# Low parts of the activations on VectorE, shorter chains, and own space for the split of h, in a hybrid attention block

## The chip, the cores and the metric

The kernel runs on one NeuronCore of a Trainium2 chip. The metric is the device time of one execution in microseconds (us), from which the median of several runs is taken. The core has five instruction queues: TensorE (PE in the profile, with its weight loads as PEld), VectorE (DVE), ScalarE (ACT), GpSimd (POOL) and SyncE (SP), which here only issues transfers. Each works its own queue in order and waits on the others through semaphores.

## What is computed

The reference is one layer of a hybrid block on x of 2048 tokens by 1024 features, in float32, cut here to what matters:

```python
u = rmsnorm(h, norm_w)
q, k, v, g, gate_lr, z, xbc, dt_raw = split_columns(u @ w_in)
gla_out = rmsnorm(gla_chunked(q, k, v, log_a), gla_norm_w) * silu(g)
xs, bm, cm = split(silu(causal_depthwise_conv(xbc)))
dt = softplus(dt_raw + dt_bias)
y = rmsnorm((ssd_chunked(xs, dt, a_neg, bm, cm) + xs * d_skip) * silu(z), ssd_norm_w)
h = h + concat(gla_out, y) @ w_out
h = h + sigmoid(rmsnorm(h, pe_norm_w) @ w_pe_gate) * (p @ w_pe)
return rmsnorm(h, final_norm_w)
```

`gla_chunked` is gated linear attention over four heads; `ssd_chunked` a state space scan over two groups of eight heads of width 64. In each chunk of the scan the state gains `B^T (x * dt * decay_to_end)`.

## The kernel before, in words

The tokens are worked in four blocks of 512 (`NB` = 4, `TB` = 512), each as four chunks of 128 (`NT` = 4). Features lie on the partitions, tokens along the free axis. Every large product is made of three passes of TensorE in a reduced float32 format: an operand is split into a **high part**, which is a copy rounded to that format, and a **low part**, the operand minus its high part, and the passes are high*high, high*low and low*high. So each activation that TensorE reads costs a copy (ScalarE) and then a subtraction that needs the copy. Weights are split in the first block (`split_w`, lines 196 and 197), written back to memory, and only loaded in the later three (`load_w`).

The steps that the change touches:
- `u_steps` (L379): the normalized input of the next block, eight pieces of 128 x 512. L386 multiplies (VectorE), L387 copies the high part (ScalarE), L389 forms the low part: GpSimd in general, VectorE for the even pieces of the first block.
- `gla_steps` (L513): one head of the gated attention. L559 and `rsqrt_tiny` give a scale per token, L563 applies it with four ScalarE passes (`on`), L569 transposes, L573 multiplies with the gate, L574 and L575 split into `mq`; L575 is GpSimd's. `mq` is read by the output projection (L878 to L880).
- `ssd_steps` (L580): one group of the scan. `make_x` (L599) transposes x of a chunk into a PSUM bank (L602), L604 (VectorE) makes `xd` = x * dt from it, L607 (GpSimd) makes `xe` = `xd` * dte, L611 (ScalarE) and L612 (GpSimd) split `xe` into `xh`. The state update L660 to L662 reads `xh`; L657 reads `xd`. `make_m` (L630) makes the decay mask, ten ScalarE passes (L634, L636) and two VectorE passes (L637) per chunk. L663 (GpSimd) scales the state.
- `ssd_norm_steps` (L676): L681, L683 and L684 normalize and split the scan's output; L684 is GpSimd's.
- `lr_steps` (L421) makes dt, the decays and `dte` in small tiles.
- The end of a block: `out_proj(ht, mqd, h_done)` (L1000) adds the last projection to h, feature tile by feature tile (d = 0 to 7). After each, `h_done` (L989) makes the high part (L995, ScalarE) and the low part (L996, VectorE) of h times a weight, and `hsq.add` squares h (L353, ScalarE) and sums the squares (L356, GpSimd). The tiles 0 to 3 go to one buffer of the tag `mq`, 4 to 7 to a second, and that tag has two buffers; at d = 4 the second one is still read as `mqd` by the projection under way. Then come the gate products (`dense_t`, L254 to L256), whose first one has the sum of squares (`sum_bc`, L320) behind its sixth feature tile (`mid`, L257).

The order of work on every engine comes from a scheduler, which starts from the order of the program and moves instructions that it holds ready past others. Side work (generators in `side`) is advanced by `step()` between the large products.

Of the kernel before, what the change touches and what calls it, by code (L numbers as in the profile page):

```python
# [35 lines left out]
def hybrid_kernel(ctx, tc, x_nat, x_t, p_t, w_t, w_n0, w_n, w_o, w_g, w_p, prm, gup, cst, out):  # L36
# [342 lines left out]
    def u_steps(b, rb, res, src=None):  # L379
        u = big.tile([P, 2, KT, TB], F32R, name="u", tag="u")  # L380
        res.append(u)
        for k in range(KT):
            xp = sb.tile([P, TB], F32, name="xp", tag="tmp", bufs=SB["tmp"])
            if src is None:
                nc.sync.dma_start(out=xp, in_=x_t[b, :, k, :])
            stt(out=xp, in0=xp if src is None else src[:, k, :], scalar=pr[:, C_NW + k:C_NW + k + 1], in1=rb, op0=ALU.mult, op1=ALU.mult)  # L386
            nc.scalar.copy(out=u[:, 0, k, :], in_=xp)  # L387
            eng = nc.gpsimd if src is None or k % 2 else nc.vector
            eng.tensor_tensor(out=u[:, 1, k, :], in0=xp, in1=u[:, 0, k, :].bitcast(F32), op=ALU.subtract)  # L389
            yield  # L390

    corr = []
# [28 lines left out]
    def lr_steps(lrn, lrT, dtr, cx):  # L421
# [49 lines left out]
        dte = sm.tile([P, NT, 16], F32, name="dte", tag="dte", bufs=1)  # L471
        tt(out=flat(dte), in0=cps[:, NS:2 * NS], in1=flat(cum), op=ALU.subtract)
        act(out=flat(dte), in_=flat(dte), func=AF.Exp)
        cx.update(dt=dt, cum=cum, elast=elast, dte=dte, cd=cd, ecd=ecd)

    def loga_steps(lrT, heads, bcs):
# [36 lines left out]
    def gla_steps(h, v, sg, fs, qm, km, mq):  # L513
# [46 lines left out]
        rs = rsqrt_tiny(ss, NT, 1.0 / 256, EPS)  # L560
        on = sb.tile([P, NT, 256], F32, name="on", tag="amh", bufs=SB["amh"])
        for t in range(NT):
            act(out=on[:, t, :], in_=rs_in[t // 2][:, (t % 2) * 256:(t % 2 + 1) * 256], func=AF.Copy,  # L563
                scale=rs[:, t:t + 1])
        yield
        for e2 in range(2):
            ps = pss.tile([P, TB], F32, name="pss")
            for t in range(NT):
                nc.tensor.transpose(out=ps[:, t * P:(t + 1) * P], in_=on[:, t, e2 * P:(e2 + 1) * P],  # L569
                                    identity=ident)  # L570
            kt = 2 * (h % 2) + e2
            og = sg[:, e2, :]
            stt(out=og, in0=ps, scalar=hgw[:, e2:e2 + 1], in1=og, op0=ALU.mult, op1=ALU.mult)  # L573
            nc.scalar.copy(out=mq[:, 0, kt, :], in_=og)  # L574
            nc.gpsimd.tensor_tensor(out=mq[:, 1, kt, :], in0=og, in1=mq[:, 0, kt, :].bitcast(F32),  # L575
                                    op=ALU.subtract)
            if e2 == 0:
                yield

    def ssd_steps(g, bt, ctl, xs, cx):  # L580
# [18 lines left out]
        def make_x(t):  # L599
            xps = pss.tile([P, TB], F32, name="pss")  # L600
            for m in range(4):
                nc.tensor.transpose(out=xps[:, m * P:(m + 1) * P], in_=xs[:, m, t * P:(t + 1) * P], identity=ident)  # L602
            xd = sb.tile([P, 8, 64], F32, name="xd", tag="xd", bufs=SB["xd"])
            tt(out=xd, in0=xps.rearrange("p (h c) -> p h c", c=64),  # L604
               in1=dt[:, t, h8].unsqueeze(2).broadcast_to([P, 8, 64]), op=ALU.mult)
            xe = sb.tile([P, 8, 64], F32, name="xe", tag="tmp", bufs=SB["tmp"])
            nc.gpsimd.tensor_tensor(out=xe, in0=xd, in1=dte[:, t, h8].unsqueeze(2).broadcast_to([P, 8, 64]),  # L607
                                    op=ALU.mult)
            xh = sb.tile([P, 2, 512], F32R, name="xh", tag="xh", bufs=SB["xh"])
            xef = xe.rearrange("p h c -> p (h c)")  # L610
            nc.scalar.copy(out=xh[:, 0, :], in_=xef)  # L611
            nc.gpsimd.tensor_tensor(out=xh[:, 1, :], in0=xef, in1=xh[:, 0, :].bitcast(F32), op=ALU.subtract)  # L612
            return xd, xh

        def load_m(t):
# [60 lines left out]
    def ssd_norm_steps(g, xs, sqs, mq):  # L676
# [3 lines left out]
        for m in range(4):  # L680
            stt(out=xs[:, m, :], in0=xs[:, m, :], scalar=pr[:, C_SW + 4 * g + m:C_SW + 4 * g + m + 1],  # L681
                in1=y, op0=ALU.mult, op1=ALU.mult)
            nc.scalar.copy(out=mq[:, 0, m, :], in_=xs[:, m, :])  # L683
            nc.gpsimd.tensor_tensor(out=mq[:, 1, m, :], in0=xs[:, m, :], in1=mq[:, 0, m, :].bitcast(F32), op=ALU.subtract)  # L684

    def final_steps(b, ht, parts, cs, deng, pool=()):
        n = cs.stop - cs.start
# [22 lines left out]
    def new_mq():  # L710
        return big.tile([P, 2, 4, TB], F32R, name="mq", tag="mq", bufs=2)
# [41 lines left out]
    for b in range(NB):  # L753
# [229 lines left out]
        if b + 1 < NB:  # L983
            gu = u_steps(b + 1, rbs.pop(), ures)
            side.append(gu)
        hw = [None, None]
        hsq = SumSq()

        def h_done(d):  # L989
            if d % 4 == 0:  # L990
                hw[d // 4] = new_mq()
            hd = ht[:, d, :]
            w = pr[:, C_PW + d:C_PW + d + 1]
            hq = hw[d // 4]
            act(out=hq[:, 0, d % 4, :], in_=hd, func=AF.Copy, scale=w)  # L995
            stt(out=hq[:, 1, d % 4, :], in0=hd, scalar=w, in1=hq[:, 0, d % 4, :].bitcast(F32),  # L996
                op0=ALU.mult, op1=ALU.subtract)
            hsq.add(hd)

        out_proj(ht, mqd, h_done)  # L1000
# [12 lines left out]
        for d, cs in jobs:  # L1013
# [6 lines left out]
            for k in range(2):  # L1020
# [3 lines left out]
                mm(out=pps, lhsT=hi[:, sl], rhs=pb[:, ks], start=(k == 0), stop=False)  # L1024
                mm(out=pps, lhsT=hi[:, sl], rhs=pl[:, ks], start=False, stop=False)
                mm(out=pps, lhsT=lo[:, sl], rhs=pb[:, ks], start=False, stop=(k == 1))
            gps = dense_t(lambda k: hw[k // 4][:, 0, k % 4, cs], lambda k: hw[k // 4][:, 1, k % 4, cs], n, gw[d],
                          None if yh else h_sum)
            if yh is None:
                yh = True  # L1030
# [101 lines left out]
```

## Time and profile before

| | us |
|---|---|
| median of 3 runs | 1877.78 (1873.1 to 1881.28) |
| the profiled execution | 1877.63 |
| its span in the profile | 1875.9 |
| PE busy | 1831.1 (98%) |
| PEld busy | 1538.6 (82%) |
| DVE busy | 1021.3 (54%) |
| ACT busy | 776.1 (41%) |
| POOL busy | 383.4 (20%) |

The span is the time from the first to the last instruction that the profile counts; the execution lasts 1.7 us longer. An engine's busy time is the union of its instructions. A matmul record lasts longer than the distance to the next, since they are pipelined, so time lost by PE is better seen in its waits and in the distances between starts. A wait names the instruction that released the engine.

### The profile page before, as it was taken

What the parts mean: (1) busy time and instruction counts of PE and PEld (TensorE: products, weight loads), DVE (VectorE), ACT (ScalarE), POOL (GpSimd) and SP (SyncE); (2) the same over time, 40 slices, a digit from 0 to 9 for tenths busy, and PEclk for the clock granted to TensorE, in tenths of its full rate; (3) what the DMA queues carried; (4) which work ended last, traced back from release to release, by engine and by line L of the source; (5) the groups of instructions that cost most, each with busy time, mean ns of one, the idle gap of its engine ahead of it and who ended that gap; (6) DMA issues with size and microseconds to landing.
All of it is one profiled execution on the core that took longest, in us unless ns stands there. A gap on an engine that the chain in (4) does not pass through costs nothing.

```text
span 1875.9 us, 25880 instructions
## 1 busy us (share of the span) xinstructions
PE 1831.1 (98%) x9674; PEld 1538.6 (82%) x9674; DVE 1021.3 (54%) x1959; ACT 776.1 (41%) x1557; POOL 383.4 (20%) x355
## 2 busy tenths in 40 slices
PE   8989999999999999999999999999999999999997
PEld 6878888877887888887788788887888888888887
DVE  8776676477566345425555544523546545551544
ACT  6575454355355334224434533313424453321431
POOL 3132012034203101204311310301420221020222
PEclk9999999999999999999999999999999999999998
DMA  7767686778785557556568556655657755666651
GB/s 271 266 214 268 225 304 217 267 245 286 256 285 162 185 164 235 161 180 214 181 225 251 154 172 197 203 176 176 217 178 264 214 157 169 182 196 187 204 174 46
DMA packets 131853, 390.60 MB, mean 208 GB/s; under 512 B 13712, under 2 KB 32400, under 8 KB 131344
## 3 DMA queue, kind: packets, MB, share of 16 engines
q1 hardware_dynamic: 129744, 382.39, 63.0%
q0 software_dynamic: 1984, 6.55, 0.9%
q8 instruction: 76, 1.25, 0.3%
q14 instruction: 49, 0.40, 0.1%
HBM read 306.58 MB, written 82.31 MB: 207 GB/s over the span
## 4 chain that ended last, share of the span: by engine, by line
PE 76%; DVE 5%; DMA 4%; ACT 3%; issue 2%; POOL 1%; SPq 0%; DVEq 0%; ACTq 0%; POOLq 0%
PE psd L256 14%; PE psd L254 14%; PE psd L255 14%; PE psd L880 5%; PE psd L879 5%; PE psd L878 5%; PE psd L277 3%; PE psd L275 3%; PE psd L279 3%; PE pss L558 1%; PE pss L657 1%; PE pss L554 1%; DMA xp<-x_t 1%; PE pss L652 1%; DMA wkl<-wk_t 1%
## 5 line engine op out<-in xcount | busy, mean ns | idle before, releaser
L254 PE MATMUL psd<-u,wkl 128*128 128x512 f32 x864 | 343.0, 397 | 0.2
L255 PE MATMUL psd<-u,wkl 128*128 128x512 f32 x864 | 337.6, 391 | 0.0
L256 PE MATMUL psd<-u,wkl 128*128 128x512 f32 x864 | 337.2, 390 | 0.0
L254 PEld LDWEIGHTS psd<-u,wkl 128*128 128x128 f32 x864 | 162.3, 188 | 34.9 <-issue 1.9
L256 PEld LDWEIGHTS psd<-u,wkl 128*128 128x128 f32 x864 | 162.2, 188 | 34.1
L255 PEld LDWEIGHTS psd<-u,wkl 128*128 128x128 f32 x864 | 162.6, 188 | 32.5 <-issue 0.7
L356 POOL TENSOR_TENSOR sq<-sq,sqt 128x512 f32<-128x512 f32 (+1 forms) x77 | 98.7, 1282 | 396.5 <-ACT sqt L353 396.5
L879 PE MATMUL psd<-mq,wkl 128*128 128x512 f32 x384 | 151.5, 395 | 1.8 <-POOL mq L575 1.7
L878 PE MATMUL psd<-mq,wkl 128*128 128x512 f32 x384 | 153.2, 400 | 0.0
L412 DVE SCALAR_TENSOR_TENSOR acc<-psd,hcw,acc 128x511 f32<-128x511 f32 x144 | 107.1, 744 | 79.7 <-ACT acc L409 77.8
L880 PE MATMUL psd<-mq,wkl 128*128 128x512 f32 x384 | 150.0, 391 | 0.0
L197 DVE TENSOR_TENSOR whl<-wraw,whl 128x512 fp32r<-128x512 f32 (+1 forms) x136 | 110.1, 816 | 52.9 <-ACT whl L196 52.7
L881 DVE TENSOR_TENSOR ht<-ht,psd 128x512 f32<-128x512 f32 x128 | 87.3, 684 | 93.9 <-PE psd L880 93.2
L634 ACT ACTIVATE em<-em,cum 128x128 f32<-128x128 f32 x256 | 83.3, 391 | 105.2 <-DMA em<-cd 99.6
L196 ACT CAST whl<-wraw 128x512 fp32r<-128x512 f32 (+1 forms) x136 | 82.2, 618 | 72.2 <-PE psd L256 26.9
L275 PE MATMUL psd<-wkl,u 128*128 128x256 f32 (+1 forms) x384 | 111.5, 290 | 0.0
L277 PE MATMUL psd<-wkl,u 128*128 128x256 f32 (+1 forms) x384 | 109.8, 286 | 0.0
L279 PE MATMUL psd<-wkl,u 128*128 128x256 f32 (+1 forms) x384 | 109.7, 286 | 0.0
L254 PE MATMUL psd<-u,whl 128*128 128x512 f32 x272 | 108.9, 400 | 0.0
L255 PE MATMUL psd<-u,whl 128*128 128x512 f32 x272 | 107.6, 396 | 0.7 <-DVE u L389 0.4
L256 PE MATMUL psd<-u,whl 128*128 128x512 f32 x272 | 107.3, 395 | 0.3 <-DVE whl L197 0.3
L575 POOL TENSOR_TENSOR mq<-sg,mq 128x512 fp32r<-128x512 f32 x32 | 43.7, 1370 | 278.5 <-ACT mq L574 278.5
(282 smaller groups left out, 3940.0 us busy)
## 6 DMA issues: line engine op xcount, KB each, us to landing
wkl<-wk_t SPq DMA_DIRECT2D x216, 512.0 KB, 4.1
wkl<-wk_o SPq DMA_DIRECT2D x96, 512.0 KB, 3.6
wk_t<-whl SPq DMA_DIRECT2D x72, 512.0 KB, 3.7
wkl<-wk_g SPq DMA_DIRECT2D x44, 512.0 KB, 3.6
wraw<-w_t SPq DMA_DIRECT2D x36, 512.0 KB, 5.0
wkl<-wk_n SPq DMA_DIRECT2D x36, 512.0 KB, 3.6
em<-cd SPq DMA_DIRECT2D x64, 256.0 KB, 4.2
wk_o<-whl SPq DMA_DIRECT2D x32, 512.0 KB, 3.6
```

What stands on the lines that cost most here:

```text
L197: tt(out=t[:, 1, :], in0=s, in1=t[:, 0, :].bitcast(F32), op=ALU.subtract)
L254: mm(out=ps, lhsT=hi[:, sl], rhs=rhi(k), start=(k == 0), stop=False)
L255: mm(out=ps, lhsT=hi[:, sl], rhs=rlo(k), start=False, stop=False)
L256: mm(out=ps, lhsT=lo[:, sl], rhs=rhi(k), start=False, stop=(k == KT - 1))
L275: mm(out=outs[t], lhsT=ug(0, k)[:, ts], rhs=hi[:, sl], start=first, stop=False, skip_group_check=True)
L277: mm(out=outs[t], lhsT=ug(0, k)[:, ts], rhs=lo[:, sl], start=False, stop=False, skip_group_check=True)
L279: mm(out=outs[t], lhsT=ug(1, k)[:, ts], rhs=hi[:, sl], start=False, stop=last, skip_group_check=True)
L356: self.eng.tensor_tensor(out=self.acc[:, cs], in0=self.acc[:, cs], in1=sq, op=ALU.add)
L412: stt(out=acc[:, s:TB], in0=ps[:, 0:TB - s], scalar=w(j), in1=acc[:, s:TB], op0=ALU.mult, op1=ALU.add)
L878: mm(out=ps, lhsT=hi[:, sl], rhs=mq[:, 0, k, :], start=(k == 0), stop=False)
L879: mm(out=ps, lhsT=hi[:, sl], rhs=mq[:, 1, k, :], start=False, stop=False)
L880: mm(out=ps, lhsT=lo[:, sl], rhs=mq[:, 0, k, :], start=False, stop=(k == 3))
```

## The change

The low parts of L389, L575, L612 and L684 and the product `xe` of L607 go from GpSimd to VectorE; the low part of the first v (L907) stays on GpSimd. `xe` is made straight from the PSUM bank, in front of `xd`, with `dte` multiplied by `dt` once in `lr_steps`. Two of the four scalings `on` (L563) go from ScalarE to VectorE. The split of h keeps one buffer of the tag `mq` for the tiles 0 to 3; the tiles 4 and 5 go to the space of `xs`, 6 to that of `bt` and `ctl`, 7 to that of `cb` and `ec`, which the scan has finished with.

```diff
--- before.py
+++ after.py
@@ -385,8 +385,7 @@
                 nc.sync.dma_start(out=xp, in_=x_t[b, :, k, :])
             stt(out=xp, in0=xp if src is None else src[:, k, :], scalar=pr[:, C_NW + k:C_NW + k + 1], in1=rb, op0=ALU.mult, op1=ALU.mult)
             nc.scalar.copy(out=u[:, 0, k, :], in_=xp)
-            eng = nc.gpsimd if src is None or k % 2 else nc.vector
-            eng.tensor_tensor(out=u[:, 1, k, :], in0=xp, in1=u[:, 0, k, :].bitcast(F32), op=ALU.subtract)
+            tt(out=u[:, 1, k, :], in0=xp, in1=u[:, 0, k, :].bitcast(F32), op=ALU.subtract)
             yield
 
     corr = []
@@ -471,6 +470,7 @@
         dte = sm.tile([P, NT, 16], F32, name="dte", tag="dte", bufs=1)
         tt(out=flat(dte), in0=cps[:, NS:2 * NS], in1=flat(cum), op=ALU.subtract)
         act(out=flat(dte), in_=flat(dte), func=AF.Exp)
+        tt(out=dte, in0=dte, in1=dt, op=ALU.mult)
         cx.update(dt=dt, cum=cum, elast=elast, dte=dte, cd=cd, ecd=ecd)
 
     def loga_steps(lrT, heads, bcs):
@@ -560,8 +560,11 @@
         rs = rsqrt_tiny(ss, NT, 1.0 / 256, EPS)
         on = sb.tile([P, NT, 256], F32, name="on", tag="amh", bufs=SB["amh"])
         for t in range(NT):
-            act(out=on[:, t, :], in_=rs_in[t // 2][:, (t % 2) * 256:(t % 2 + 1) * 256], func=AF.Copy,
-                scale=rs[:, t:t + 1])
+            o = rs_in[t // 2][:, (t % 2) * 256:(t % 2 + 1) * 256]
+            if t < 2:
+                act(out=on[:, t, :], in_=o, func=AF.Copy, scale=rs[:, t:t + 1])
+            else:
+                nc.vector.tensor_scalar_mul(out=on[:, t, :], in0=o, scalar1=rs[:, t:t + 1])
         yield
         for e2 in range(2):
             ps = pss.tile([P, TB], F32, name="pss")
@@ -572,8 +575,7 @@
             og = sg[:, e2, :]
             stt(out=og, in0=ps, scalar=hgw[:, e2:e2 + 1], in1=og, op0=ALU.mult, op1=ALU.mult)
             nc.scalar.copy(out=mq[:, 0, kt, :], in_=og)
-            nc.gpsimd.tensor_tensor(out=mq[:, 1, kt, :], in0=og, in1=mq[:, 0, kt, :].bitcast(F32),
-                                    op=ALU.subtract)
+            tt(out=mq[:, 1, kt, :], in0=og, in1=mq[:, 0, kt, :].bitcast(F32), op=ALU.subtract)
             if e2 == 0:
                 yield
 
@@ -600,16 +602,15 @@
             xps = pss.tile([P, TB], F32, name="pss")
             for m in range(4):
                 nc.tensor.transpose(out=xps[:, m * P:(m + 1) * P], in_=xs[:, m, t * P:(t + 1) * P], identity=ident)
+            xp3 = xps.rearrange("p (h c) -> p h c", c=64)
+            xe = sb.tile([P, 8, 64], F32, name="xe", tag="tmp", bufs=SB["tmp"])
+            tt(out=xe, in0=xp3, in1=dte[:, t, h8].unsqueeze(2).broadcast_to([P, 8, 64]), op=ALU.mult)
             xd = sb.tile([P, 8, 64], F32, name="xd", tag="xd", bufs=SB["xd"])
-            tt(out=xd, in0=xps.rearrange("p (h c) -> p h c", c=64),
-               in1=dt[:, t, h8].unsqueeze(2).broadcast_to([P, 8, 64]), op=ALU.mult)
-            xe = sb.tile([P, 8, 64], F32, name="xe", tag="tmp", bufs=SB["tmp"])
-            nc.gpsimd.tensor_tensor(out=xe, in0=xd, in1=dte[:, t, h8].unsqueeze(2).broadcast_to([P, 8, 64]),
-                                    op=ALU.mult)
+            tt(out=xd, in0=xp3, in1=dt[:, t, h8].unsqueeze(2).broadcast_to([P, 8, 64]), op=ALU.mult)
             xh = sb.tile([P, 2, 512], F32R, name="xh", tag="xh", bufs=SB["xh"])
             xef = xe.rearrange("p h c -> p (h c)")
             nc.scalar.copy(out=xh[:, 0, :], in_=xef)
-            nc.gpsimd.tensor_tensor(out=xh[:, 1, :], in0=xef, in1=xh[:, 0, :].bitcast(F32), op=ALU.subtract)
+            tt(out=xh[:, 1, :], in0=xef, in1=xh[:, 0, :].bitcast(F32), op=ALU.subtract)
             return xd, xh
 
         def load_m(t):
@@ -681,7 +682,7 @@
             stt(out=xs[:, m, :], in0=xs[:, m, :], scalar=pr[:, C_SW + 4 * g + m:C_SW + 4 * g + m + 1],
                 in1=y, op0=ALU.mult, op1=ALU.mult)
             nc.scalar.copy(out=mq[:, 0, m, :], in_=xs[:, m, :])
-            nc.gpsimd.tensor_tensor(out=mq[:, 1, m, :], in0=xs[:, m, :], in1=mq[:, 0, m, :].bitcast(F32), op=ALU.subtract)
+            tt(out=mq[:, 1, m, :], in0=xs[:, m, :], in1=mq[:, 0, m, :].bitcast(F32), op=ALU.subtract)
 
     def final_steps(b, ht, parts, cs, deng, pool=()):
         n = cs.stop - cs.start
@@ -983,18 +984,29 @@
         if b + 1 < NB:
             gu = u_steps(b + 1, rbs.pop(), ures)
             side.append(gu)
-        hw = [None, None]
+        hq = [None] * KT
         hsq = SumSq()
 
+        def h_tiles(d):
+            if d == 0:
+                t = new_mq()
+                for k in range(4):
+                    hq[k] = (t[:, 0, k, :], t[:, 1, k, :])
+            elif d == 4:
+                t = sb.tile([P, 2, 2, TB], F32R, name="hx", tag="xs", bufs=SB["xs"])
+                for k in range(2):
+                    hq[4 + k] = (t[:, 0, k, :], t[:, 1, k, :])
+            elif d >= 6:
+                hq[d] = tuple(sb.tile([P, TB], F32R, name="hs", tag=tag, bufs=SB[tag])
+                              for tag in (("bt", "ctl"), ("cb", "ec"))[d - 6])
+
         def h_done(d):
-            if d % 4 == 0:
-                hw[d // 4] = new_mq()
+            h_tiles(d)
             hd = ht[:, d, :]
             w = pr[:, C_PW + d:C_PW + d + 1]
-            hq = hw[d // 4]
-            act(out=hq[:, 0, d % 4, :], in_=hd, func=AF.Copy, scale=w)
-            stt(out=hq[:, 1, d % 4, :], in0=hd, scalar=w, in1=hq[:, 0, d % 4, :].bitcast(F32),
-                op0=ALU.mult, op1=ALU.subtract)
+            hi, lo = hq[d]
+            act(out=hi, in_=hd, func=AF.Copy, scale=w)
+            stt(out=lo, in0=hd, scalar=w, in1=hi.bitcast(F32), op0=ALU.mult, op1=ALU.subtract)
             hsq.add(hd)
 
         out_proj(ht, mqd, h_done)
@@ -1024,7 +1036,7 @@
                 mm(out=pps, lhsT=hi[:, sl], rhs=pb[:, ks], start=(k == 0), stop=False)
                 mm(out=pps, lhsT=hi[:, sl], rhs=pl[:, ks], start=False, stop=False)
                 mm(out=pps, lhsT=lo[:, sl], rhs=pb[:, ks], start=False, stop=(k == 1))
-            gps = dense_t(lambda k: hw[k // 4][:, 0, k % 4, cs], lambda k: hw[k // 4][:, 1, k % 4, cs], n, gw[d],
+            gps = dense_t(lambda k: hq[k][0][:, cs], lambda k: hq[k][1][:, cs], n, gw[d],
                           None if yh else h_sum)
             if yh is None:
                 yh = True
```

## Rows read from the trace of the kernel before

**Rows 1.** The page: busy time, share of the span and instructions of each engine.

```profile
PE 1831.1 (98%) x9674; PEld 1538.6 (82%) x9674; DVE 1021.3 (54%) x1959; ACT 776.1 (41%) x1557; POOL 383.4 (20%) x355
```

**Rows 2.** Waits of PE, whole span: total us, times, longest.

```profile
PE psd L275 <- ACT whl L196: 6.6, 2, 6.3
PE pss L661 <- POOL xh L612: 2.7, 4, 0.9
PE pss L660 <- ACT xh L611: 2.3, 4, 0.7
...
PE psd L879 <- POOL mq L575: 2.2, 4, 0.6
...
PE pss L517 <- DVE ec L665: 2.1, 2, 1.4
PE psd L254 <- ACT mq L995: 2.1, 1, 2.1
...
PE pss L569 <- ACT on L563: 1.8, 3, 0.8
...
PE pss L320 <- POOL sq L356: 0.8, 2, 0.4
PE psd L255 <- DVE mq L996: 0.8, 1, 0.8
```

**Rows 3.** Busy per stretch, first block: length, engines, PEclk, DMA share, GB/s.

```profile
110.00:120.00 10.00, 8.49 (x44) 6.23 (x43) 4.92 (x13) 5.80 (x15) 4.42 (x3) 0.83 0.81 272
...
420.00:440.00 20.00, 17.02 (x65) 12.36 (x64) 17.20 (x18) 11.20 (x19) 12.06 (x9) 0.90 0.85 301
```

**Rows 4.** Timeline, a state update of the second block: start, us, instruction, [idle before].

```profile
588.95 0.50 PE L660 MATMUL pss<-xh,bn 128*128 128x512 f32 x1 [0.57 <-ACT xh L611]
...
589.29 0.40 PE L255 MATMUL psd<-u,wkl 128*128 128x512 f32 x1
...
590.30 0.50 PE L661 MATMUL pss<-xh,bn 128*128 128x512 f32 x1 [0.62 <-POOL xh L612]
...
590.64 0.40 PE L662 MATMUL pss<-xh,bn 128*128 128x512 f32 x1
...
590.88 0.39 PE L256 MATMUL psd<-u,wkl 128*128 128x512 f32 x1
```

**Rows 5.** Groups of VectorE by line: busy, mean ns, idle before.

```profile
L197 DVE TENSOR_TENSOR whl<-wraw,whl 128x512 fp32r<-128x512 f32 x132 | 107.1, 818 | 52.5 <-ACT whl L196 52.4
...
L604 DVE TENSOR_TENSOR xd<-pss,dt 128x512 f32<-128x512 f32 x32 | 21.9, 685 | 3.7 <-PE pss L602 3.7
```

**Rows 6.** Groups of GpSimd by line.

```profile
L612 POOL TENSOR_TENSOR xh<-xe,xh 128x512 fp32r<-128x512 f32 x32 | 41.7, 1303 | 30.5 <-ACT xh L611 30.5
...
L607 POOL TENSOR_TENSOR xe<-xd,dte 128x512 f32<-128x512 f32 x32 | 38.0, 1189 | 173.5 <-DVE xd L604 169.6 <-DVE fs L499 3.9
```

**Rows 7.** Groups of ScalarE by line.

```profile
L634 ACT ACTIVATE em<-em,cum 128x128 f32<-128x128 f32 x256 | 83.3, 391 | 105.2 <-DMA em<-cd 99.6 <-PE psd L256 5.4
...
L563 ACT ACTIVATE on<-pss,yy 128x256 f32<-128x256 f32 x64 | 25.0, 474 | 24.7 <-DVE yy L302 24.7
```

**Rows 8.** Timeline, the end of the projection in the first block.

```profile
434.46 0.68 DVE L881 TENSOR_TENSOR ht<-ht,psd 128x512 f32<-128x512 f32 x1
...
435.10 2.56 ACT L995 ACTIVATE mq<-ht,pr 128x512 fp32r<-128x512 f32 x4
...
435.85 4.29 DVE L996 SCALAR_TENSOR_TENSOR mq<-ht,pr,mq 128x512 fp32r<-128x512 f32 x4 [0.71 <-ACT mq L995]
...
439.65 2.08 PE L320 MATMUL pss<-sq,cf 128*128 128x512 f32 x2
```

**Rows 9.** Busy per stretch, scan of the second block (columns as in Rows 3).

```profile
570.00:580.00 10.00, 10.00 (x69) 8.54 (x68) 7.50 (x13) 4.68 (x13) 3.85 (x4) 1.00 0.59 178
```

**Rows 10.** Timeline, the first block: a GpSimd and a VectorE instruction side by side.

```profile
422.80 1.73 POOL L389 TENSOR_TENSOR u<-xp,u 128x512 fp32r<-128x512 f32 x1
...
423.31 1.78 DVE L996 SCALAR_TENSOR_TENSOR mq<-ht,pr,mq 128x512 fp32r<-128x512 f32 x1
```

## The prediction

> **What bounds the kernel now.** I read the page first: PE is busy for 1831.1 of the span's 1875.9 us, VectorE for 54%, GpSimd for 20% [rows 1]. So TensorE's own work is the floor, and no edit here touches it; whatever the change brings must come out of the 44.8 us in which PE does nothing. The waits of PE say whose they are [rows 2]: 6.6 us are the first weights, which nobody can hurry here, and the rest is small pieces of 0.4 to 2.1 us spread over the four blocks. Of them the change addresses the two waits on the split of `xe` (2.7 and 2.3), the one on `mq` of L575 (2.2), the one on `on` (1.8), the two on the split of h (2.1 and 0.8) and the one on the squares (0.8). Third, the timeline around one such wait, because an entry understates what it costs: L255 starts 0.34 us after L660, where 0.24 is usual (L662 to L256), and L661 starts 1.01 after L255 though its wait counts 0.62 [rows 4]. That is 0.1 + (1.01 - 0.24 - 0.62) = 0.25 us on top of each wait. Fourth, the granted clock: it is 0.83 in one stretch of 10 us that holds such waits, and 0.90 in the 20 us around the end of the first block's projection [rows 3].
>
> **The change, part by part.** All is set against the profiled execution of 1877.63 us, which stands at the median of 1877.78. A measurement of this kernel can tell about 0.5%, or 9.4 us, from no change.
>
> *`xe` and its split.* A chunk's chain before is `xd` 0.69 (L604), `xe` 1.19 (L607), the ScalarE copy, the low part 1.30 (L612) [rows 5, 6]. After it is `xe` from the bank, 0.69, the same copy, and a low part of 0.69 if VectorE takes as long for it as for L604, whose width is the same; `xd` fits beside the copy. The high part comes 1.19 us earlier and the low part 1.19 + 0.61 = 1.80. The longest waits are 0.7 and 0.9 [rows 2], so all eight should go: **-5.0 us**.
>
> *`on`.* Four ScalarE passes of 0.474 in a row, 1.90 us [rows 7], become two and two side by side. Even if VectorE is no faster than ScalarE, the chain is 0.95 us shorter, and the longest wait was 0.8 [rows 2]: **-1.8**.
>
> *L575.* The low part goes from about 1.30 to 0.69, but on VectorE it has to queue behind the gate's second product, which GpSimd ran past. Bounds 0 and 2.2; I take half, **-1.1**.
>
> *L389 and L684.* PE's waits name neither [rows 2], so I give nothing; the next large product and the rest of the projection cover them. Without that cover, each such wait would cost about a VectorE pass, 0.69.
>
> *The split of h.* In the first block PE waits for the tiles 4 to 7 because their buffer is still `mqd`. Own space lets 4, 5 and 6 be split as their sums arrive. But what is late next is the sum of squares, which PE meets at the sixth tile: it needs the last tile's L881, a copy and a square on ScalarE of 2.56 / 4 = 0.64 each, and a GpSimd pass of 1.3. L881 ended at 435.14 [rows 8], so the sum could start at 435.14 + 0.64 + 0.64 + 1.3 = 437.7 plus handoffs, instead of 439.65: a gain of 1.8. Against it, three of the four L996 (4.29 / 4 = 1.07 each [rows 8]) now stand in front of that L881 on a VectorE that is busy for 17.20 of 20 us there [rows 3]; all 3.2 us in front would make the sum 1.4 late. I take -0.2, between the two. In the later blocks no weights are split, VectorE has room, and the wait on the squares goes: -0.8. Together **-1.0**, with ends of +0.6 and -2.6. The 2.9 us of waits on L995 and L996 are not counted: they only move to the sum.
>
> *The refills.* Waits that disappear: eight on `xe`, three on `on`, two on the squares, about two on L575. 15 x 0.25 = **-3.8**.
>
> *The clock.* 10 us at 0.83 are 3.4 us at the lower level (1.2 instead of 2.4 GHz), which cost 1.7 us of work. PE was waiting for `xe` in this stretch, so I let this one go: **-1.7**. The stretch at 0.90 is 4.0 us at the lower level, worth up to 2.0; the wait before it stays in another form, so it stays.
>
> *What is added.* 124 low parts and 32 `xe` at 0.69 are 107 us on VectorE, 32 scalings at no more than 0.474 are 15, four small products of `dte` are under 1 and lie far ahead of their use: VectorE goes from 1021 to about 1143 us, 61%. Some comes back: L996 beside a GpSimd L389 took 1.78 us [rows 10] where the four of rows 8 average 1.07, and 156 GpSimd passes leave. That load lies under PE. What lies on the path is the PSUM bank of `xe`: it is read twice now, so each is released 0.69 us later. PE waits on such a release in L517 (2 times, 2.1 us) [rows 2]. Bounds: nothing, and 32 x 0.69 = 22. Nearest the row, I prolong those two and as many more: 4 x 0.69 = **+2.7**.
>
> *New space and queues.* No transfer is added or moved. The tiles of h wait for the scan's last readers, which the projection in front needs anyway; the next block's `xs`, `bt`, `ctl`, `cb` and the `ec` load on SP wait for the last gate product, and the first large product of v covers that.
>
> Sum: -5.0 - 1.8 - 1.1 - 1.0 - 3.8 - 1.7 + 2.7 = -11.7, so **1865.9**, rounded to 1866.
>
> **The rivals.** *VectorE stands in order (about no change).* A low part waits for ScalarE's copy, and what is behind it on VectorE waits too; GpSimd could stand idle at no cost. The Trainium skill, TensorE: Matmul & The Clock Gate, gives VectorE a strict first-in-first-out queue in its table at the top; the rows agree, as L197 holds VectorE idle. For it: L197, the low part that VectorE already has, stood 52.4 us in 132 executions, 0.40 us each [rows 5]. 124 x 0.40 = 49 us of standing; if PE needs what is behind in one case of four, 12.3 us, and the time is 1878. Against: VectorE has 46% to spare, and most of L197's standing is found with nothing else to do.
>
> *No faster on VectorE (a small gain).* The GpSimd passes that stay hold VectorE up as rows 10 show, 1.78 for 1.07. A new low part of 0.69 + 0.7 is then as long as GpSimd's 1.30 [rows 6], and the terms of `xe`, of L575 and ten refills fall away: 11.7 - 5.0 - 1.1 - 2.5 = 3.1, giving 1874.5. Against: the sums of squares, the main GpSimd work that stays, lie mostly in other stages than the scan. The Trainium skill, Perfetto Trace Analysis, section Optimizing Scalar/DVE Operations, warns in this sense that offloading between GpSimd and VectorE might not help, since they share a read port; rows 10 agree that they hold each other up.
>
> *VectorE becomes PE's bound in the scan (slower).* There VectorE is busy for 7.50 of 10 us [rows 9], and a chunk gains 2 x 0.69 = 1.4 us. The copy of `xe` shares ScalarE with the eight passes of the decay mask, 8 x 0.391 = 3.1 us [rows 7]. If the copy falls behind them, the low part holds VectorE for that long, with the mask's own products behind it. In 12 of the 32 chunks that is 37 us, giving 1866 + 37 = 1903; from 7 chunks on (22 us) the time is over 1887. Against: `xe` is ready 1.19 us earlier, and the program asks for the copy first.
>
> That the change doesn't do what it says could only be in the space for h, if its tiles wait for old readers; these are done before the projection starts.
>
> **How the numbers follow.** Forecast 0.56 (1858 to 1871, of which 0.04 lies above 1868.4), VectorE in order 0.20, no faster 0.12, slower 0.12. Faster by over 0.5% is 0.52; within it 0.04 + 0.20 + 0.12 = 0.36; slower 0.12. The low end takes the better bounds: 11.7 + 1.1 on L575 + 1.6 on h + 2.7 of the bank + 2.0 of clock = 19.1, or 1858.5, and 2.5 us for stalls of VectorE that I don't see: 1856. The high end takes in the two middle rivals: 1880.
>
> **What would show it.** PE's waits without L612, L563 and L996; L611 following a VectorE `xe`; POOL busy down by more than the 79.7 us of rows 6, and DVE up by some 100; L995 for the tiles 4 to 6 before the projection ends; PE waiting for L320 in the first block still. It is wrong if PE's waits name VectorE's low parts for more than some 5 us in sum, if L517 or L509 wait for `xd`, or if the granted clock falls in more stretches than before.

## The result and the profile after

| | before | after |
|---|---|---|
| median, us | 1879.5 (1873.1 to 1881.3, 4 runs) | 1856.9 (1852.0 to 1859.3, 4 runs) |
| profiled execution, us | 1877.6 | 1852.0 |
| its span, us | 1875.9 | 1850.2 |

The ratio is 0.9876 with a 95% interval of 0.9856 to 0.9897: faster by 22.6 us, where 11.7 were forecast. Direction and range were right; the size is twice that of the sum.

The page of after, busy time of each engine, against [rows 1]:

```profile
PE 1820.3 (98%) x9674; PEld 1536.9 (83%) x9674; DVE 1082.9 (59%) x2151; ACT 764.0 (41%) x1525; POOL 174.8 (9%) x199
```

GpSimd is down by 208.6 us, as the change says. VectorE is up by 61.6 only, where 122 were forecast: something was given back. The waits of PE after, against [rows 2]:

```profile
PE psd L275 <- ACT whl L196: 6.9, 2, 6.5
...
PE pss L572 <- ACT on L565: 1.8, 3, 0.9
...
PE psd L1036 <- DVE gth L1045: 1.6, 1, 1.6
...
PE pss L517 <- DVE ec L666: 0.6, 1, 0.6
```

The waits on `xh`, on the low part in `mq` of the old L575 and on the split of h are gone. That on `on` (L565) has not moved, and one on the gate's result (L1045) has grown from 0.2 us to 1.6. Over all entries of this view PE waited 37.5 us in 41 waits before and 22.8 in 23 after: 14.7 us less. Eighteen waits fewer at the 0.25 of [rows 4] make another 4.5, by estimate. The rest is the clock. The mean granted clock of the span, before and then after:

```profile
die 0 (median of its cores): 1875.9 us, clock 0.994
```

```profile
die 0 (median of its cores): 1850.2 us, clock 0.997
```

A clock of 0.994 means that about 2 x 0.006 x 1875.9 = 22.5 us were spent at 1.2 instead of 2.4 GHz; after it is about 11.1. Where the clock had fallen is seen per stretch (columns as in [rows 3]), two more stretches and the end of before, then after:

```profile
125.00:135.00 10.00, 7.96 (x33) 6.19 (x32) 7.03 (x21) 5.68 (x16) 1.81 (x2) 0.83 0.59 210
430.00:450.00 20.00, 17.02 (x57) 11.58 (x56) 13.53 (x16) 13.29 (x21) 7.52 (x6) 0.83 0.77 269
...
1860.00:1875.90 15.90, 5.00 (x32) 3.90 (x30) 8.07 (x26) 1.25 (x3) 1.95 (x3) 0.70 0.40 132
```

```profile
110.00:120.00 10.00, 10.00 (x65) 7.86 (x64) 8.36 (x19) 7.24 (x18) 2.73 (x1) 1.00 0.58 185
125.00:135.00 10.00, 9.34 (x46) 7.55 (x45) 8.36 (x21) 8.46 (x20) 0.00 (x0) 1.00 0.92 329
420.00:440.00 20.00, 17.95 (x74) 13.30 (x73) 15.37 (x23) 13.29 (x22) 2.42 (x2) 1.00 0.79 275
430.00:450.00 20.00, 18.18 (x79) 14.46 (x78) 14.59 (x23) 10.59 (x19) 2.57 (x2) 1.00 0.74 267
...
1840.00:1850.20 10.20, 1.22 (x2) 0.50 (x2) 5.02 (x19) 0.00 (x0) 0.00 (x0) 0.52 0.31 103
```

The column before the last two is the clock. Both kernels spend some 10 us at the lower level at their end, where TensorE has little left to do; for the difference that does not count. Before, it was below 1 in three more places: 2 x 0.17 x 10 = 3.4 us at the lower level at 110 and again at 125, and 2 x 0.17 x 20 = 6.8 from 430 to 450, which cost up to 13.6 / 2 = 6.8 us. Ahead of them PE had waited 0.7 and 0.9 us for `xh`, 2.0 for a step of `rsqrt_tiny` (L290), and 2.1 for the split of h. After, it is 1.00 over the whole of the first 1830 us. So 14.7 + 4.5 + 6.8 = 26.0, where the two spans differ by 25.7. The prediction let go of the first stretch of [rows 3] alone.

Why VectorE's busy time rose so little, by its groups after (mean ns of one behind the bar), against [rows 5]:

```profile
L197 DVE TENSOR_TENSOR whl<-wraw,whl 128x512 fp32r<-128x512 f32 x132 | 92.8, 710 | 35.9 <-ACT whl L196 33.5 <-DMA xp<-x_t 2.1
...
L613 DVE TENSOR_TENSOR xh<-xe,xh 128x512 fp32r<-128x512 f32 x32 | 22.1, 691 | 16.7 <-ACT xh L612 16.4
...
L578 DVE TENSOR_TENSOR mq<-sg,mq 128x512 fp32r<-128x512 f32 x32 | 21.7, 689 | 9.3 <-ACT mq L577 8.6
```

The new low parts take 0.69 us, as forecast from L604. And L197, which the change doesn't touch, went from 818 to 710 ns: 132 x 0.108 = 14.3 us from one line. Added up pass by pass in the two traces, the lines that VectorE had before take some 48 us less. (The rest of the gap to 122 is that passes in a row overlap in the record, which the busy time counts once.)

The end of the first block's projection after (timeline), against [rows 8]:

```profile
419.69 0.68 DVE L882 TENSOR_TENSOR ht<-ht,psd 128x512 f32<-128x512 f32 x1
...
420.41 0.73 ACT L1008 ACTIVATE hs<-ht,pr 128x512 fp32r<-128x512 f32 x1 [0.39 <-DVE ht L882]
...
421.80 1.46 POOL L356 TENSOR_TENSOR sq<-sq,sqt 128x512 f32<-128x512 f32 x1 [0.84 <-ACT sqt L353]
...
422.03 1.78 DVE L1009 SCALAR_TENSOR_TENSOR hs<-ht,pr,hs 128x512 fp32r<-128x512 f32 x1
...
423.31 1.12 PE L320 MATMUL pss<-sq,cf 128*128 128x512 f32 x2
```

The last sum of h is there at 419.69 instead of 434.46: 14.8 us of the gain lie ahead of it, in the first block. The sum of squares follows it by 3.62 us, where it was 5.19. The pair in the middle shows what is left: a VectorE pass of 1.78 beside a GpSimd pass.

### The profile page after: what moved, and what is told of

It reads as the page before. It is cut to its first block, busy times and chain, and to the rows that moved or that the text cites. A ratio compares the mean times of both kernels' runs of the same rounds, so it can differ in the third digit from the quotient of the medians.

```text
span 1850.2 us, 25852 instructions
## 1 busy us (share of the span) xinstructions
PE 1820.3 (98%) x9674; PEld 1536.9 (83%) x9674; DVE 1082.9 (59%) x2151; ACT 764.0 (41%) x1525; POOL 174.8 (9%) x199
## 4 chain that ended last, share of the span: by engine, by line
PE 86%; DVE 5%; DMA 4%; ACT 3%; issue 2%; SPq 0%; DVEq 0%; ACTq 0%
PE psd L255 15%; PE psd L256 15%; PE psd L254 15%; PE psd L879 6%; PE psd L881 5%; PE psd L880 5%; PE psd L277 3%; PE psd L279 3%; PE psd L275 3%; DMA em<-cd 2%; PE pss L558 2%; PE pss L658 2%; PE pss L653 1%; PE pss L554 1%; PE pss L320 1%
## 5 line engine op out<-in xcount | busy, mean ns | idle before, releaser
L197 DVE TENSOR_TENSOR whl<-wraw,whl 128x512 fp32r<-128x512 f32 (+1 forms) x136 | 95.7, 711 | 36.7 <-ACT whl L196 34.3
L196 ACT CAST whl<-wraw 128x512 fp32r<-128x512 f32 (+1 forms) x136 | 81.9, 618 | 72.3 <-PE psd L256 22.8
L881 PEld LDWEIGHTS psd<-mq,wkl 128*128 128x128 f32 x384 | 72.1, 188 | 15.5 <-issue 0.5
```

Source lines behind the costliest of these rows:

```text
L197: tt(out=t[:, 1, :], in0=s, in1=t[:, 0, :].bitcast(F32), op=ALU.subtract)
L881: mm(out=ps, lhsT=lo[:, sl], rhs=mq[:, 0, k, :], start=False, stop=(k == 3))
```

## The experiments

Two theories. Theory 1, **chains**: each part is worth the waits of PE that name it, with their refills and the clock. Theory 2, **shared access**: a GpSimd pass that reads beside a VectorE pass lengthens it, as [rows 10] show, and the delay reaches PE under other names; what counts is that such passes go. Each kernel was timed beside the kernel before on the same chip, and kernels that were not timed side by side are compared by their ratios to it (95% intervals in brackets).

**The space for h alone** (h_only, on the kernel before), and the change **without it** (h_back):

```diff
-        hw = [None, None]
+        hq = [None] * KT
...
-                hw[d // 4] = new_mq()
+            h_tiles(d)
```

> The kernel before, with the own space for the split of h alone. Theory 1, chains: each part of the change removes the PE waits of its own chain and the half clock behind them; here the waits on L995, L996 and on the squares, 3.7 us in the waits view, with the stretch of clock 0.90 in the first block: 6 to 9 us faster than before, some 1871 to 1873. Theory 2, the shared access: what counted was taking GpSimd passes away from beside VectorE; VectorE stays as held up as before, so the last tile's sum stays late and the gain is 2 us or less.

> The changed kernel with the split of h in two buffers of the tag mq as before. Theory 1, chains: the wait on L995 at the end of the first block's projection returns and with it a stretch of half clock: 5 to 8 us slower than the changed kernel. Theory 2, the shared access: VectorE is ahead now, the split of the last four tiles is quick, at most 2 us slower.

Measured: 1880.55 us, ratio 1.0007 [0.9996, 1.0019], and for the second 1857.96, ratio 0.9884 [0.9868, 0.9900] against the change's 0.9876. Either way the space is worth no more than some 2 us. Two waits of PE in h_only say why:

```profile
PE pss L517 <- DVE ec L665: 4.3, 4, 1.6
...
PE psd L1035 <- DVE gth L1044: 2.6, 1, 2.6
```

The waits on the split went, and PE now waits 2.6 us for a gate result behind it, where it was 0.2, and 4.3 instead of 2.1 for `ec`. Theory 1 is wrong here.

**The four low parts alone** (low_only, on the kernel before):

```diff
-            eng = nc.gpsimd if src is None or k % 2 else nc.vector
-            eng.tensor_tensor(out=u[:, 1, k, :], in0=xp, in1=u[:, 0, k, :].bitcast(F32), op=ALU.subtract)
+            tt(out=u[:, 1, k, :], in0=xp, in1=u[:, 0, k, :].bitcast(F32), op=ALU.subtract)
...
-            nc.gpsimd.tensor_tensor(out=xh[:, 1, :], in0=xef, in1=xh[:, 0, :].bitcast(F32), op=ALU.subtract)
+            tt(out=xh[:, 1, :], in0=xef, in1=xh[:, 0, :].bitcast(F32), op=ALU.subtract)
```

(L575 and L684 likewise.) And the change **with these four back on GpSimd** (lows_back), the same lines the other way.

> The kernel before, with the four low parts (of u, of the gated attention, of xe, of the scan's output) on VectorE and nothing else; xe itself stays a GpSimd pass behind xd. Theory 1, chains: half of the wait on xe and most of that on L575, some 4 us and their refills, 4 to 7 us faster than before. Theory 2, the shared access: most of the whole gain, 12 to 18 us, with VectorE's own lines at their short durations (L681 near 0.75 us where it had 1.01).

> The changed kernel with the four low parts back on GpSimd: own space for h and the short chains (xe from the bank, on shared) remain. Theory 1, chains: the waits on L995 and L996 and on the high part of xe stay away, those on L612 and L575 come back in part: 14 to 17 us faster than before, 6 to 8 slower than the changed kernel. Theory 2, the shared access: 5 to 9 us faster than before, the rest of the gain is lost.

Measured: low_only 1862.85 us, ratio 0.9913 [0.9897, 0.9928], 16.4 us faster than before; lows_back 1867.4, ratio 0.9936 [0.9923, 0.9949], 12.0 faster than before and 11 slower than the change. The first is in Theory 2's range and far above Theory 1's; the second lies between the two. Low parts are most of it, but the short chains are worth more than Theory 2 gave them.

**Two low parts at a time**: L389 and L684 (uy_only), and L575 and L612 (xm_only), each on the kernel before with the edit shown above. PE's waits before name L575 and L612; of the other two they name L389 alone, and that for 0.4 us:

```profile
PE psd L255 <- POOL u L389: 0.4, 2, 0.2
```

> Before, with the low parts of L389 and L684 alone on VectorE (28 + 32 passes of GpSimd go). PE's waits before name neither of them. Theory 1 (chains: a part is worth the waits of PE that name it, with their refills): 0, within 1.5 us of before, because the waits on xh, on the mq of L575 and on `on` all stay. Theory 2 (shared access: GpSimd passes that run beside VectorE lengthen VectorE's passes, and that delay reaches PE under other names): these two lines lengthened VectorE's passes by about as much as L575 and L612 together, so it should be a good part of the 16.5 us of all four, 5 to 9 us faster, with waits on xh or mq shorter though nothing in their chains was edited.

> Before, with the low parts of L575 and L612 alone on VectorE. Theory 1 (chains): these two carry the waits of PE that went, so nearly the whole 16.5 us of all four low parts, 13 to 17 us faster. Theory 2 (shared access): about the half that the other two lines leave, 6 to 10 us faster, with the first product of each new block (L275, L509, L517) still late beside L389's GpSimd passes.

Measured: uy_only 1874.18, ratio 0.9961 [0.9949, 0.9973], 7.3 us faster; xm_only 1866.0, ratio 0.9923 [0.9911, 0.9935], 14.5 faster. The first is in Theory 2's range and speaks against Theory 1, which gave 0; the second is in Theory 1's range, not in Theory 2's. Together they are 21.8, more than the 16.4 of both at once; whether the two overlap isn't settled, since the profiled executions add up (5.1 + 9.1 = 14.2 against 16.2 by the spans 1870.8, 1866.8 and 1859.7). In uy_only VectorE's lines got shorter, L197 from 818 to 758 ns and L681, the pass that runs beside L684, from 1007 to 747. But the gain is hardly in waits by name: 36.4 us in 41 waits stand in its profile, 37.5 in 41 before. Of the waits that Theory 2 would see shorter, those on `xh` and on the `mq` of L575 stayed within 0.4 us, and those on the split of h, in `mq` too, went (2.9) though nothing in that chain was edited; but those on `ec` and `xs` grew from 4.2 to 7.2. Most of what the profiled execution gained is clock, by its stretches:

```profile
110.00:120.00 10.00, 8.49 (x45) 6.25 (x44) 4.89 (x13) 5.79 (x15) 4.19 (x3) 0.83 0.80 270
125.00:135.00 10.00, 9.75 (x53) 7.61 (x50) 8.96 (x24) 8.47 (x23) 2.92 (x2) 1.00 0.66 218
...
415.00:450.00 35.00, 33.43 (x136) 26.21 (x135) 29.93 (x40) 22.26 (x37) 9.04 (x6) 0.95 0.85 287
```

That is 3.4 + 3.5 = 6.9 us at the lower level where before had 13.6, worth 3.4; with 1.1 of waits it makes 4.5 of the 5.1 between the two spans. Over the runs the clock is worth less: the six have a mean of 0.9950, the eleven of before beside them 0.9938, so 18.7 instead of 23.3 us at the lower level, or 2.3. Where the rest of the 7.3 lies stays open.

**The reading, without a chain** (shadow): the change, with a GpSimd subtraction put back behind each low part, on the source that nothing reads any more; its result is unused. And **the same load that only writes** (shadow_ms): three fills in its place. The edit is shown for L612; at the other three it is alike.

```diff
             tt(out=xh[:, 1, :], in0=xef, in1=xh[:, 0, :].bitcast(F32), op=ALU.subtract)
+            nc.gpsimd.tensor_tensor(out=xef, in0=xef, in1=xh[:, 0, :].bitcast(F32), op=ALU.subtract)
```

```diff
             tt(out=xh[:, 1, :], in0=xef, in1=xh[:, 0, :].bitcast(F32), op=ALU.subtract)
+            nc.gpsimd.memset(xef, 0.0)
+            nc.gpsimd.memset(xef, 0.0)
+            nc.gpsimd.memset(xef, 0.0)
```

> The changed kernel, with a GpSimd pass of the same size put behind each of the 124 low parts that VectorE now forms (it subtracts in place on the source, which nothing reads after that, so its result is unused). GpSimd's load beside VectorE is then that of before, but no chain of PE goes through GpSimd. Theory 1 (chains): 0 to 2 us slower than the changed kernel, about 1858. Theory 2 (shared access): VectorE's busy time up by 25 us or more and the time up by 6 to 12 us, about 1863 to 1869.

> The changed kernel with GpSimd work behind the same 124 low parts, but work that only writes: three fills with zero of the dead source (0.52 us each by the fills of L519, 1.57 us together, where the subtraction took about 1.28), unused again. GpSimd's queue and the source's buffer are held for as long or longer than with the subtraction. If the 15 us of the subtractions came from queueing on GpSimd or from buffers that come free late, this gives them back too: 1870 to 1877. If they came from reading beside VectorE (Theory 2), VectorE's passes keep their length (busy time within 10 us of the changed kernel's) and the time stays within 4 us of it: 1856 to 1861.

Measured: shadow 1874.0, ratio 0.9957 [0.9945, 0.9969], 15 us slower than the change and above Theory 2's range; shadow_ms 1855.3, ratio 0.9878 [0.9862, 0.9894], the same as the change. Their pages, shadow first:

```profile
PE 1826.3 (98%) x9674; PEld 1537.6 (82%) x9674; DVE 1132.4 (61%) x2151; ACT 765.2 (41%) x1525; POOL 365.9 (20%) x323
```

```profile
PE 1821.1 (98%) x9674; PEld 1535.2 (83%) x9674; DVE 1085.2 (59%) x2151; ACT 765.0 (41%) x1525; POOL 366.1 (20%) x571
```

GpSimd is busy for the same time in both, and VectorE runs the same 2151 instructions; with readers beside it they take 47 us more than with writers. By group, L197 and L386, shadow first:

```profile
L197 DVE TENSOR_TENSOR whl<-wraw,whl 128x512 fp32r<-128x512 f32 x132 | 104.9, 803 | 35.4 <-ACT whl L196 35.2
...
L386 DVE SCALAR_TENSOR_TENSOR xp<-xp,pr,urb 128x512 f32<-128x512 f32 x24 | 27.9, 1163 | 14.0 <-DMA xp<-x_t 14.0
```

```profile
L197 DVE TENSOR_TENSOR whl<-wraw,whl 128x512 fp32r<-128x512 f32 x132 | 92.0, 705 | 36.3 <-ACT whl L196 36.2
...
L386 DVE SCALAR_TENSOR_TENSOR xp<-xp,pr,urb 128x512 f32<-128x512 f32 x24 | 23.3, 970 | 15.5 <-DMA xp<-x_t 15.4
```

And one place of shadow in order of time:

```profile
418.19 1.75 POOL L356 TENSOR_TENSOR sq<-sq,sqt 128x512 f32<-128x512 f32 x1
...
418.71 0.68 DVE L887 TENSOR_TENSOR ht<-ht,psd 128x512 f32<-128x512 f32 x1
...
420.87 1.44 POOL L356 TENSOR_TENSOR sq<-sq,sqt 128x512 f32<-128x512 f32 x1 [0.93 <-ACT sqt L353]
...
421.08 1.78 DVE L1014 SCALAR_TENSOR_TENSOR hx<-ht,pr,hx 128x512 fp32r<-128x512 f32 x1
```

L887, which takes one operand from a PSUM bank, keeps its 0.68 beside GpSimd; L1014, with both large operands in SBUF, takes 1.78. How the delay reaches PE, by three waits of shadow:

```profile
PE psd L256 <- DVE whl L197: 4.1, 5, 2.0
PE pss L320 <- POOL sq L356: 3.6, 2, 2.5
...
PE pss L320 <- DVE sq L356: 2.4, 3, 0.8
```

None of the three names an added pass. In the change they are 1.0, 0 and 0, with the fills 0.5, 2.1 and 0; over all entries PE waits 36.8 us in shadow, 26.1 with the fills and 22.8 in the change. This is Theory 2. A busy queue or a late buffer is excluded as the cause, since the fills keep GpSimd busy for as long behind the same low parts and cost no time that can be told. So is another order of work: TensorE's 9674 instructions stand in the same order in all three traces. The subtraction also holds its second operand, the high part, which the fills don't touch; but in shadow's trace no instruction of PE, VectorE or ScalarE waits for one of the added passes, and PE waits for no transfer. The Trainium skill, SBUF — State Buffer, section Who interferes with whom, says that a VectorE instruction with two SBUF inputs contends with a GpSimd instruction that reads SBUF, and not with one that only writes it; these rows agree.

**The sums of squares on VectorE too** (sq_dve, on the change), **all of `on` as well** (sq_on_dve), and **the state's scaling as well** (no_pool):

```diff
-            self.eng = eng or nc.gpsimd
+            self.eng = eng or nc.vector
...
-            if t < 2:
-                act(out=on[:, t, :], in_=o, func=AF.Copy, scale=rs[:, t:t + 1])
-            else:
-                nc.vector.tensor_scalar_mul(out=on[:, t, :], in0=o, scalar1=rs[:, t:t + 1])
+            nc.vector.tensor_scalar_mul(out=on[:, t, :], in0=o, scalar1=rs[:, t:t + 1])
...
-            nc.gpsimd.tensor_tensor(out=S3, in0=S3, in1=elast[:, t, h8].unsqueeze(2).broadcast_to([P, 8, 64]),
+            tt(out=S3, in0=S3, in1=elast[:, t, h8].unsqueeze(2).broadcast_to([P, 8, 64]),
                                     op=ALU.mult)
```

> The changed kernel, with the sums of squares (L356) on VectorE instead of GpSimd; GpSimd keeps next to nothing but L663. Theory 1 (chains): the wait on the squares (2.5 us, now the last VectorE pass behind it) shrinks by the half of a GpSimd pass each time, 0 to 2 us faster; against it more work on a VectorE that is full at the ends of blocks. Theory 2 (shared access): VectorE's passes beside L356 get back their length, VectorE's busy time rises by less than the 64 x 0.69 us that it takes over, and the time falls by 2 to 5 us.

> The changed kernel with the sums of squares and all four `on` on VectorE. Against the one with the squares alone there (1851.9), Theory 1 (chains): the wait on `on` (2.5 us there) goes, 2 to 4 us faster, unless VectorE, now four passes in a row of 0.48 instead of two and two, is the later of the two: then 0 to 2 slower. Theory 2 says nothing on this one beyond 0, as no GpSimd pass moves.

> As the last, and the scaling of the scan's state (L664, 32 GpSimd passes, 37.4 us in the changed kernel) on VectorE too, so that GpSimd reads next to nothing. Theory 2 (shared access): VectorE gets back some 5 us of length there, and gives 32 x 0.69 = 22 us of its own; the gain has shrunk with each step, 0 to 2 us faster. Theory 1 (chains): the scaling now stands in VectorE's order between the products of the scan that PE waits for (ec), 1 to 4 us slower.

Measured: sq_dve 1851.91, ratio 0.9843 [0.9830, 0.9856]; sq_on_dve 1851.18, ratio 0.9854 [0.9838, 0.9870]; no_pool 1855.36, ratio 0.9879 [0.9862, 0.9897]. With the squares, VectorE's passes get their length back as Theory 2 said: L386 of sq_dve is

```profile
L386 DVE SCALAR_TENSOR_TENSOR xp<-xp,pr,urb 128x512 f32<-128x512 f32 x24 | 17.9, 748 | 6.2 <-DMA xp<-x_t 5.9
```

against 928 ns in the change. VectorE took over 77 passes and its busy time rose by 29.7 us, to 1112.6. This version beats the kernel before, and the changed one by 0.33% or 6 us if the two ratios are set against each other; the two were not timed side by side, and their intervals meet at 0.9856, so a gain over the change is likely but not shown. The rest of `on` brings nothing that the intervals can tell (0.7 us faster by the medians, 2 slower by the ratios), though its wait is gone. Scaling the state on VectorE is 4.7 us slower by the ratios than without it, the way that Theory 1 said, slightly above its range; in no_pool PE waits for `ec`, the scan's product that now stands behind the scaling:

```profile
PE pss L517 <- DVE ec L663: 2.2, 3, 1.1
...
PE pss L509 <- DVE ec L663: 1.4, 3, 0.8
```

That is 3.6 us, where it was 1.7 in sq_on_dve. But all waits of PE together are 23.6 us against 23.0, and the clock fell for 6.8 us (0.83 from 120 to 140) in the profiled execution of no_pool against 3.4 in the other. So this step costs time; that it does so because the moved pass stands in PE's chain is argued from `ec`, not shown.

**`xe` as before** (xe_back, on the change; `xd` comes first again, and `dte` is not multiplied by `dt`):

```diff
-            tt(out=xe, in0=xp3, in1=dte[:, t, h8].unsqueeze(2).broadcast_to([P, 8, 64]), op=ALU.mult)
...
+            nc.gpsimd.tensor_tensor(out=xe, in0=xd, in1=dte[:, t, h8].unsqueeze(2).broadcast_to([P, 8, 64]),
+                                    op=ALU.mult)
```

> The changed kernel with `xe` made as before: `xd` first, then `xe` from it on GpSimd. The prediction gave 5.0 us and eight refills of 0.25 to the chain of `xe` as a whole, and took 2.7 back for the bank that is read twice. Theory 1 (chains): the high part comes 1.19 us later, so the 2.3 us of waits on it return with their refills, less the bank: 2 to 4 us slower, 1859 to 1861. Theory 2 (shared access): the low part on VectorE was what counted; 32 GpSimd passes come back that in the kernel before lengthened VectorE's by little (2 us), so 0 to 2 us slower and no wait on xh.

Measured: 1861.85, ratio 0.9911 [0.9896, 0.9926], 5 to 7 us slower than the change (by the medians and by the ratios). Both theories gave less. Of its waits of PE:

```profile
PE pss L516 <- DVE ec L666: 3.7, 4, 1.8
...
PE pss L661 <- ACT xh L612: 1.2, 3, 0.7
```

Only 1.2 us are on `xh`; the larger return is on `ec`, a later VectorE pass of the scan. Whether that comes from the GpSimd pass, its readers or the order on VectorE wasn't separated.

## Why the prediction was right in direction and short in size

By the ratios, 16.4 us are the low parts (low_only), 6.6 `xe` from the bank (xe_back against the change) and 1.5 the space of h (h_back), 24.5 in sum against the measured 22.6. The division depends on the order: taken back from the change, the low parts are worth 11 (lows_back). The two scalings of `on` have no run of their own.

The measured median lies 0.9 us above the low end of the range, 1856. That end had 2.5 us in it "for stalls of VectorE that I don't see", with no row behind them, and without them the range would have missed; that the number fell inside is in part luck. Of the signs named, three did not come: `on` kept its wait, PE does not wait for the squares at L320 in the first block, and VectorE rose by 61.6, not some 100. Step by step:

- **"Whatever the change brings must come out of the 44.8 us".** PE's idle time fell from 44.8 to 29.9 us, its busy time by 10.8 as well. The second is near the 4.5 + 6.8 estimated above for the refills and the clock, in which PE counts as busy.
- **L389 and L684, "I give nothing".** The step that failed most: 7.3 us (uy_only). "PE's waits name neither" holds for L684 and, but for 0.4 us, for L389; it was not enough, because these passes delay VectorE's own. The prediction had the row for it, [rows 10], and used it only for a rival and for VectorE's load.
- **The clock, -1.7.** About 6.8: all of before's falls ahead of its end went, not one. The stretch at 0.90 was kept because "the wait before it stays in another form". Over 415 to 450 us of before, h_only, low_only and the change:

```profile
415.00:450.00 35.00, 32.02 (x123) 23.96 (x122) 26.70 (x32) 22.07 (x36) 15.51 (x11) 0.90 0.84 295
```

```profile
415.00:450.00 35.00, 32.55 (x132) 25.22 (x131) 25.57 (x31) 23.03 (x38) 15.44 (x11) 0.95 0.84 301
```

```profile
415.00:450.00 35.00, 30.62 (x124) 23.57 (x123) 28.26 (x38) 20.79 (x34) 8.46 (x6) 0.95 0.81 276
```

```profile
415.00:450.00 35.00, 32.22 (x134) 24.50 (x133) 26.37 (x38) 20.52 (x33) 6.77 (x5) 1.00 0.84 298
```

  Neither the space for h nor the low parts alone kept the clock up there; the change with either taken back has 0.95 (h_back) and 0.90 (lows_back), and all five other traces with both and without the readers of shadow have 1.00 (shadow itself 0.95). In the change the sum of squares follows the last sum of h 5.19 - 3.62 = 1.6 us sooner, where 0.2 was forecast. Each kernel has one trace, so this is a pattern over traces and not a measured effect.
- **`xe` and its split, -5.0.** The waits on `xh` are gone, as forecast, but the low part on VectorE does nearly all of that (low_only). Making `xe` from the bank is worth 5 to 7 us more, through `ec`.
- **The bank read twice, +2.7.** It didn't come: L517 waits 0.6 us on `ec`, not 2.1. In the changed kernel reading it twice is 5 to 7 us cheaper than the GpSimd pass that it replaces (xe_back).
- **L575, -1.1.** The whole 2.2 went.
- **`on`, -1.8.** It stays at 1.8 us in 3 waits. The two passes left on ScalarE queue behind the decay mask, which was waiting for its load (timeline of the change):

```profile
1489.38 0.88 DVE L567 TENSOR_SCALAR on<-pss,yy 128x256 f32<-128x256 f32 x2
...
1490.44 0.40 ACT L635 ACTIVATE em<-em,cum 128x128 f32<-128x128 f32 x1 [0.38 <-DMA em<-cd]
...
1491.27 0.82 ACT L565 ACTIVATE on<-pss,yy 128x256 f32<-128x256 f32 x2
...
1491.77 0.20 PEld L572 LDWEIGHTS pss<-cf,on 128*128 128x128 f32 x2 [1.29 <-ACT on L565]
```

  VectorE's half was done at 1490.26, ScalarE's began at 1491.27. The prediction counted the length of the chain, not what its engine has in front of it. The other two of the three waits were not followed up.
- **The split of h, -1.0.** Right within what can be measured. The next late thing was sought at the sum of squares; it was a gate result behind that, 2.6 us in h_only and 1.6 in the change.
- **The refills, -3.8.** Eighteen waits fewer, 4.5 by the same 0.25, which was not measured again.
- **VectorE's load, 1143.** It is 1082.9, mostly since the passes that were stretched beside GpSimd got shorter (some 48 us); the prediction said "some comes back" and put no number to it.

Of the rivals, "VectorE stands in order" is not what this change meets: the new low parts do stand (16.7 us before L613, 9.3 before L578), but L197 stands for less than before, 35.9 us instead of 52.5, and PE waits for less. The 4.7 us of no_pool may be of this kind. "No faster on VectorE" had the interference right and its sign wrong: it let the low parts suffer from the GpSimd passes that stay, where the larger matter was that 156 of them went. The warning it took from the Trainium skill, Perfetto Trace Analysis, section Optimizing Scalar/DVE Operations, that offloading between the two might not help, stands there behind advice on a saturated VectorE; here VectorE was busy for 54%, the work moved the other way, and it did help. "VectorE becomes PE's bound" needed waits on the copy of `xe`; PE's waits after name no `xh`.

## What to carry to other kernels

Before a GpSimd pass is called free because no wait names it, look at the VectorE lines that run beside it: a line whose mean stands well above what it takes with GpSimd nearly empty (L197: 818 ns against 690 in sq_dve, where GpSimd is busy for 74.8 us) is paying for it, and that delay surfaces under other names and in the clock. To tell such a cost from a queue, put back the same load once as a pass that reads and once as one that only writes. Measure each further pass that you move: the last one here, which stands in front of a product that TensorE waits for, cost 4.7 us.

## What the runs showed of the hardware that was not expected

The interference goes both ways and is large for a single pair: VectorE's 0.75 us pass takes 1.78 beside a reading GpSimd pass, and GpSimd's own 1.29 becomes 1.44 to 1.75. It does not touch a VectorE pass with one operand in PSUM (0.68 beside GpSimd), nor does a GpSimd fill cause it (L197 at 705 ns beside 124 x 3 fills). Counted over whole traces, for VectorE's tensor-tensor passes (products, sums and differences) of 128 x 512: in before, 222 with both operands in SBUF met no GpSimd pass and took 0.69 us in the mean; 68 met a reading one for over 0.3 us and took 1.14; 78 with one operand in PSUM met one for as long and took 0.68, none over 0.70. In shadow_ms 89 with both operands in SBUF met a fill for as long and took 0.68.

The clock may gain as well. In uy_only the mean granted clock of the runs was 0.9950 instead of 0.9938, though the edit touched next to nothing that PE waited for by name (0.994 to 0.996 against 0.992 to 0.996, so the runs overlap and this is not shown).
